# A mixture-of-experts stage: a side computation tied to its written places in the queues, its vectors on GpSimd alone, and two more weight buffers

## The chip, the cores and the metric

One core of one Trainium2 chip runs the whole program. The metric is device time in microseconds (us) from launch to end, the median of several runs. Times inside the program are counted from the start of the profiled span.

## The reference, cut to what matters

The program is two transformer-like blocks over 512 tokens of width 1024. The first block ends in a mixture of 16 experts in which each expert picks its 64 best tokens. The second block has an attention layer, two feed-forward layers and a state-space layer (S5). The part that the change touches is the mixture, and the S5 layer's constant operators, which depend on weights alone and are computed while the mixture runs:

```python
def expert_choice_moe(h, p):
    B, T, D = h.shape
    cap = EC_CAPACITY * T // N_EXPERTS
    affinity = jax.nn.softmax((h @ p['router_w']).astype(jnp.float32), axis=-1)
    gates, idx = lax.top_k(jnp.swapaxes(affinity, 1, 2), cap)
    xe = jax.vmap(lambda hb, ib: hb[ib])(h, idx)
    hid = jax.nn.silu(jnp.einsum('becd,edf->becf', xe, p['exp_w1'])) * jnp.einsum('becd,edf->becf', xe, p['exp_w3'])
    ye = jnp.einsum('becf,efd->becd', hid, p['exp_w2']) * gates[..., None].astype(h.dtype)
    return jax.vmap(lambda ib, yb: jnp.zeros((T, D), yb.dtype).at[ib.reshape(-1)].add(yb.reshape(-1, D)))(idx, ye)
```

Everything is float32. The three weight matrices of the 16 experts are 384 tiles of 128x2048, 1 MB each, and every one is used once.

## The kernel before, in words

`moe` (L1515) takes the experts in eight pairs (`j` from 0 to 7; the text counts them from one, so pair two is `j == 1`). A pair needs 48 weight tiles. The first 32 belong to its **up phase**: two experts, four blocks `fb` each, four tiles `kq` to a block; TensorE multiplies the 64 gathered tokens by each tile (L1588), ScalarE evacuates the block (L1599), four transposes (L1540) and two VectorE operations (L1544, L1545) make the gated hidden layer. Between the tiles of the first expert stand eight matmuls that add the pair before into the output (`combine`, L1552), between those of the second the gather of the next pair's tokens (L1508). The last 16 tiles are the pair's **down phase** (L1620), eight steps `q` of two tiles.

The weight tiles come in one after the other on SyncE's queue (`pair_weight`, L1330, and L1533). Each goes into the next buffer of a ring, and SyncE's queue stands still until the matmuls that read the tile before it in that buffer are done. Pair one has 15 buffers. When it is over they are given up except for six, so pairs two and three have six; from pair four on, `late` adds six more and the tiles go to the two pools in turn.

`s5_prep` (L2013) is a Python generator that writes the S5 operators' work piece by piece: two exponentials and two sines, nine powers of a complex number, squares, a division (all on 128x32 elements, VectorE and ScalarE), and then for each of eight groups `q` the `vectors` (some 20 element-wise operations on up to 128x576 elements that make `CA`, `W` and `bd`) and the `products` (TensorE: two sets of four transposes of `W`, L2110, and one set of matmuls of `CA` and `bd`, L2118; each evacuated by ScalarE and, for `W`, stored to memory). The vectors of even groups are on VectorE (tiles `cuv`, `bigv`, `Wincv`, `bbdv`), those of odd groups on GpSimd (`cug`, `bigg`, `Wincg`, `bbdg`). `moe` takes a piece at twelve points of a pair, from pair two on, and whatever is left at the start of pair four.

The written place of a piece binds nothing: a scheduler at build time sorts each engine's instructions by its own estimate of when they are ready. The engines then work through their queues strictly in order. What the S5 pieces make is first read long after the mixture, in the second feed-forward stretch.

Of the kernel before, what the change touches and what calls it, by code (L numbers as in the profile page):

```python
# [28 lines left out]
NEXP, DEXP, CAP = 16, 2048, 64  # L29
DFF = 2816  # L30
TWO_PI = 2.0 * math.pi
MAGIC = 12582912.0
# [145 lines left out]
class K:  # L178
# [148 lines left out]
    def mod_cols(self, src, which, dst, bias, pool, gate=None, post=None, tags=("wa",)):  # L327
# [26 lines left out]
        if gate is not None:  # L354
            a, row = gate
            g = dst[:, a:a + 8]
            if post is not None:
                t = pool.tile([P, 8], F32, name="gcl", bufs=1)
                V.tensor_tensor(t, g, post, op=OP.mult)
                g = t  # L360
            pt = self.psum(self.mtag, 2)
            nc.tensor.transpose(pt[:8, :P], g, self.ident)
            r = pool.tile([8, P], F32, name="grw8", bufs=1)
            nc.scalar.activation(r, pt[:8, :P], AF.Copy)
            nc.gpsimd.dma_start(row, r)

    def background(self, *parts):
# [1147 lines left out]
    def moe(self):  # L1515
        nc, I = self.nc, self.I
        NJ = NEXP // 2
        with self.mes:
            with ExitStack() as es:
# [3 lines left out]
                nxt = next(g0)  # L1523
                prep, late, acc, MG = (), None, None, None
                turn = cycle(range(2))

                def weight(x):
                    if j == 0:
                        return self.first_w[x] if x < len(self.first_w) else self.pair_weight(j, x)
                    if late is None or next(turn):  # L1530
                        return self.pair_weight(j, x)
                    w = late.tile([P, 2048], F32, name="we", tag="we", bufs=6)
                    nc.sync.dma_start(w, self.weight_src(j, x))  # L1533
                    return w

                def gated(hs, hT, fb):
# [29 lines left out]
                for j in range(NJ):  # L1566
                    XG = nxt
                    last = j == NJ - 1
                    if j == 3:
                        for _ in prep:  # L1570
                            pass
                        s5s.close()
                        late = self.pool(es, "late", side="right")
                    hid = []
                    for e in range(2):
# [4 lines left out]
                        for fb in range(4):  # L1580
                            ps = self.psum("mm", 2)
                            for kq in range(4):
                                next(g0, 0)
                                w = weight(16 * e + 4 * fb + kq).rearrange("p (a b c) -> p a b c", a=2, b=2)
                                for i in range(2):
                                    k = 2 * kq + i
                                    for h in range(2):
                                        nc.tensor.matmul(ps[64 * h:64 * h + 64], XG[:, k, CAP * e:CAP * e + CAP], w[:, i, h],  # L1588
                                                         start=(k == 0), stop=(k == KD - 1), skip_group_check=True)
                                if kq == 0:  # L1590
                                    run()
                                    if e:
                                        nxt = next(gat, None) or nxt
                                else:
                                    next(comb, None)
                                if j and (kq == 0 or kq == 2 and fb % 2):
                                    next(prep, None)
                            hs = wk.tile([P, 512], F32, name="hs")
# [13 lines left out]
                    for q in range(8):  # L1612
# [3 lines left out]
                        for i in range(2):  # L1616
                            f = 2 * q + i
                            for n in range(2):
                                for h in range(2):
                                    nc.tensor.matmul(py[n][64 * h:64 * h + 64], hid[h][:, f], ww[h][:, i, 512 * n:512 * n + 512],  # L1620
                                                     start=(f == 0), stop=(f == 15), skip_group_check=True)
                        if q == 0:
# [8 lines left out]
                    if j == 0:  # L1631
# [7 lines left out]
                        for n in range(2):  # L1639
# [5 lines left out]
                            nc.scalar.activation(MG[:, 512 * n:512 * n + 512], pg, AF.Copy)  # L1645
                        if "D" in self.dbg:
                            prep = self.s5_prep(self.pool(s5s, "s5p", side="right"))
                            next(prep)
# [363 lines left out]
    def s5_prep(self, wk):  # L2012
# [14 lines left out]
        def t32(name):  # L2027
            return wk.tile([P, NPR], F32, name=name)
        are, aim = a[:, 0], a[:, 1]
        dt, dec, th, sn, cn, hp = t32("dt"), t32("dec"), t32("th"), t32("sn"), t32("cn"), wk.tile([P, 1], F32, name="hp")  # L2030
        rw = wk.tile([P, 3, NPR], F32, name="rho")
# [4 lines left out]
        nc.scalar.activation(dec, dec, AF.Exp)  # L2036
        V.tensor_tensor(th, aim, dt, op=OP.mult)
        self.sin_reduce(th, wk, [P, NPR], "s")
        V.memset(hp, math.pi / 2)
        nc.scalar.activation(sn, th, AF.Sin)  # L2040
        nc.scalar.activation(th, th, AF.Abs)
        nc.scalar.activation(cn, th, AF.Sin, scale=-1.0, bias=hp)
        pw = wk.tile([P, 2, 9, NPR], F32, name="pw")
        V.memset(pw[:, 0, 0], 1.0)
# [4 lines left out]
        for j in range(2, 9):  # L2049
            for o, sub in ((0, True), (1, False)):  # L2050
                V.tensor_tensor(t1, pw[:, 0, j - 1], pw[:, o, 1], op=OP.mult)
                V.tensor_tensor(t2, pw[:, 1, j - 1], pw[:, 1 - o, 1], op=OP.mult)
                V.tensor_tensor(pw[:, o, j], t1, t2, op=OP.subtract if sub else OP.add)
        pk = wk.tile([P, 2, 8, NPR], F32, name="pk")
        V.tensor_copy(pk[:, 0], pw[:, 0, 1:])
        V.tensor_scalar(pk[:, 1], pw[:, 1, 1:], -1.0, None, op0=OP.mult)
        nc.scalar.dma_start(self.s5p[:, 0:512], pk.rearrange("p r j n -> p (r j n)"))

        self.square(V, (cn, sn), (t1, t2), wk)
        self.square(V, (t1, t2), (cn, sn), wk)  # L2060
        self.square(V, (cn, sn), (rw[:, 1], rw[:, 2]), wk)
        nc.scalar.dma_start(self.s5p[:, 512:], rw.rearrange("p a n -> p (a n)"))
        den, nr, cre, cim = t32("den"), t32("nr"), t32("cre"), t32("cim")
        V.tensor_tensor(den, are, are, op=OP.mult)
        V.tensor_tensor(t1, aim, aim, op=OP.mult)
        V.tensor_tensor(den, den, t1, op=OP.add)
        V.reciprocal(den, den)
        V.tensor_scalar(nr, pw[:, 0, 1], 1.0, None, op0=OP.subtract)
        ni = pw[:, 1, 1]
        V.tensor_tensor(t1, nr, are, op=OP.mult)  # L2070
# [9 lines left out]
        for q in range(0, NPR, 16):  # L2080
            s = slice(q, q + 16)
            self.cmul((V, G)[q // 16], wk, bb[:, 0, s, None], bb[:, 1, s, None], [v[:, s, None, None] for v in (cre, cim)],
                 [b[:, r, s, None, :] for r in range(2)], [P, 16, 1, 16])
        KT = wk.tile([P, KD, 8, 16], F32, name="KT", tag="sb")

        def vectors(q):

            E, t = ((V, "v"), (G, "g"))[q % 2]
            s = slice(NQ * q, NQ * q + NQ)
# [33 lines left out]
        yield  # L2123
        ops = None
        for q in range(KD + 1):
            new = vectors(q) if q < KD else None
            yield
            if ops is not None:
                yield from products(q - 1, *ops)
            ops = new  # L2130
        nc.gpsimd.dma_start(self.s5k[:, :, 112:].rearrange("q p x -> p q x"), KT.rearrange("p q j c -> p q (j c)"))
# [247 lines left out]
```

## Time and profile before

| what | us |
|---|---|
| median of 3 runs | 3420.55 (3420.32 to 3424.09) |
| the profiled execution, its own time | 3418.57 |
| its span, first to last instruction | 3416.5 |
| pair one of the mixture begins (first L1588) | 984.2 |
| pair two begins | 1103.35 |
| pair two's up phase ends, down phase begins | 1252.38 |
| pair three begins | 1290.86 |
| the last expert's last weight matmul | 2011 |

The core's 16 DMA engines carry all transfers. In most of the mixture they move 421 GB/s, which is a 1 MB (1.0486 MB) weight tile every 2.49 us. TensorE's granted clock is given as a share of 2.4 GHz: 1.00 is 2.4 GHz, 0.50 is 1.2 GHz.

### The profile page before, as it was taken

The page shows a single profiled execution, that of the slowest core. Times are in us where ns is not written, and L with a number is a line of the kernel's source. Part 1 is how long each engine was busy: PE and PEld are TensorE (multiplying, and loading weights), DVE is VectorE, ACT ScalarE, POOL GpSimd, SP SyncE. Part 2 cuts the span into 40 slices and gives each one's busy share as a digit, 9 for nine tenths or more (in the row PEclk, how much of TensorE's full clock was granted, in tenths as well). Part 3 has the DMA queues.
Part 4 walks back from the last instruction along what each step waited for, and adds up shares of the span by engine and source line. Part 5 has one row for each costly group of instructions (what it writes and reads, how often), then busy time and mean ns, then how long its engine had stood idle before and what let it go on. Part 6 is the DMA issues. An engine that isn't in the chain of part 4 may idle for free.

```text
span 3416.5 us, 41161 instructions
## 1 busy us (share of the span) xinstructions
PE 3156.0 (92%) x15981; PEld 1962.0 (57%) x15981; DVE 1727.5 (51%) x3088; ACT 961.3 (28%) x1799; POOL 688.6 (20%) x721
## 2 busy tenths in 40 slices
PE   8988999999999689999999989899888998999999
PEld 3746566666564233333333247565767777778887
DVE  3656767665451911101110136786577775556464
ACT  3314444443221111011001022236332332234242
POOL 1022234432110720000000023210496002210000
PEclk9999989899899899999999999789999998999999
DMA  5643211111659689999999965310336465422221
GB/s 216 240 162 113 66 44 47 44 38 65 246 217 380 242 307 414 419 421 421 421 421 421 421 259 187 111 68 1 120 130 205 164 216 139 152 81 96 96 99 68
DMA packets 144586, 681.34 MB, mean 199 GB/s; under 512 B 25455, under 2 KB 33815, under 8 KB 76424
## 3 DMA queue, kind: packets, MB, share of 16 engines
q1 hardware_dynamic: 134480, 652.47, 50.1%
q0 software_dynamic: 5536, 18.16, 1.4%
q10 hardware_dynamic: 4376, 8.09, 0.7%
q8 instruction: 126, 2.06, 0.2%
q14 instruction: 68, 0.56, 0.1%
HBM read 654.54 MB, written 24.12 MB: 199 GB/s over the span
## 4 chain that ended last, share of the span: by engine, by line
PE 39%; DMA 19%; POOL 7%; DVE 7%; issue 2%; ACT 2%; SPq 0%; POOLq 0%; ACTq 0%; DVEq 0%
DMA we<-in_w_dram 18%; PE mm L1588 5%; PE mm L284 5%; PE mm L285 5%; PE mm L286 5%; POOL cug L2000 3%; PE ch L1620 2%; POOL sca L2001 2%; PE sm L286 1%; PE sm L285 1%; PE sm L284 1%; PE tr L1508 1%; DMA wa<-in_adaw_dram 1%; PE ch L284 1%; PE ch L286 1%
## 5 line engine op out<-in xcount | busy, mean ns | idle before, releaser
L1588 PE MATMUL mm<-we,XG 128*64 128x512 f32 x2048 | 482.6, 609 | 4.6 <-DMA we<-in_w_dram 3.7
L284 PE MATMUL mm<-hh,wh 128*128 128x512 f32 x704 | 281.9, 401 | 21.0 <-DVE vg L1954 16.5
L1588 PEld LDWEIGHTS mm<-we,XG 128*64 128x64 f32 x2048 | 135.4, 138 | 278.8 <-issue 255.4
L1620 PE MATMUL ch<-we,hid 128*64 128x512 f32 x1024 | 267.0, 600 | 16.8 <-DMA we<-in_w_dram 16.7
L285 PE MATMUL mm<-hl,wh 128*128 128x512 f32 x704 | 277.9, 395 | 0.0
L286 PE MATMUL mm<-hh,wl 128*128 128x512 f32 x704 | 272.4, 395 | 0.0
L1544 DVE SCALAR_TENSOR_TENSOR hth<-hth,tr 128x256 f32<-128x256 f32 x64 | 26.9, 420 | 399.5 <-ACT hth L1543 398.9
L1620 PEld LDWEIGHTS ch<-we,hid 128*64 128x64 f32 x1024 | 96.4, 136 | 180.2 <-issue 131.8
L1557 DVE TENSOR_TENSOR acc<-acc,sm 128x512 f32<-128x512 f32 x48 | 33.0, 687 | 305.4 <-PE sm L1552 305.4
L284 PEld LDWEIGHTS mm<-hh,wh 128*128 128x128 f32 x704 | 134.3, 191 | 63.7 <-issue 27.3
L346 DVE SCALAR_TENSOR_TENSOR macc<-wa,cvs,macc 128x512 f32<-128x512 f32 (+1 forms) x119 | 153.6, 1306 | 17.7 <-DMA wa<-in_adaw_dram 15.6
L1669 POOL TENSOR_TENSOR ess<-ess,mhalf 128x1 f32<-128x1 f32 x4 | 2.9, 716 | 786.5 <-DVE ess L1668 786.4
L1599 ACT ACTIVATE hs<-mm 128x512 f32<-128x512 f32 x64 | 38.2, 597 | 415.5 <-PE mm L1588 402.6
L279 DVE TENSOR_TENSOR wl<-wu,wh 128x1024 fp32r<-128x1024 f32 x88 | 115.4, 1313 | 75.2 <-ACT wh L278 74.9
L286 PEld LDWEIGHTS mm<-hh,wl 128*128 128x128 f32 x704 | 134.2, 191 | 29.4
L285 PEld LDWEIGHTS mm<-hl,wh 128*128 128x128 f32 x704 | 134.7, 191 | 26.8 <-POOL hl L455 0.5
L461 POOL TENSOR_TENSOR X<-X,gy 128x512 f32<-128x512 f32 x20 | 28.2, 1430 | 589.3 <-DVE gy L1686 589.2
L278 ACT ACTIVATE wh<-wu 128x1024 fp32r<-128x1024 f32 x88 | 93.3, 1060 | 129.4 <-PE mm L285 96.7
L279 DVE TENSOR_TENSOR wl<-wd,wh 128x1024 fp32r<-128x1024 f32 (+1 forms) x48 | 56.1, 1171 | 96.2 <-ACT wh L278 96.2
L284 PE MATMUL mm<-hTh,wh 128*128 128x512 f32 x208 | 90.4, 435 | 6.5 <-ACT th L795 5.5
L278 ACT ACTIVATE wh<-wd 128x1024 fp32r<-128x1024 f32 (+1 forms) x48 | 47.5, 989 | 164.9 <-PE sm L286 75.0
L286 PE MATMUL mm<-hTh,wl 128*128 128x512 f32 x208 | 89.7, 431 | 2.8 <-DVE wl L279 2.8
(845 smaller groups left out, 6787.7 us busy)
## 6 DMA issues: line engine op xcount, KB each, us to landing
we<-in_w_dram SPq DMA_DIRECT2D x384, 1024.0 KB, 19.8
wu<-in_wupf_dram SPq DMA_DIRECT2D x44, 1024.0 KB, 4.8
wa<-in_adaw_dram SPq DMA_DIRECT2D x24, 1024.0 KB, 4.9
wa<-in_adaw_dram SPq DMA_DIRECT2D x96, 256.0 KB, 4.2
wa<-in_modw_dram SPq DMA_DIRECT2D x16, 1024.0 KB, 6.2
wd<-in_wdn_dram SPq DMA_DIRECT2D x16, 1024.0 KB, 4.8
aw<-in_awin_dram SPq DMA_DIRECT2D x12, 1024.0 KB, 4.9
wi<-in_win_dram SPq DMA_DIRECT2D x46, 256.0 KB, 2.6
```

Of the source, the lines that this page charges most:

```text
L278: self.nc.scalar.activation(h, x, AF.Copy)
L279: (E or self.nc.vector).tensor_tensor(l, x, h.bitcast(F32), op=OP.subtract)
L284: mm(ps, a[0], b[0], start=start, stop=False)
L285: mm(ps, a[0], b[1], start=False, stop=False)
L286: mm(ps, a[1], b[0], start=False, stop=stop)
L346: V.scalar_tensor_tensor(a, w, c, a, op0=OP.mult, op1=OP.add)
L1508: nc.tensor.matmul(ps[:, c * i:c * i + c], self.xn[:, t, o:o + P], oh[:, t], start=(t == 0), stop=(t == TT - 1), skip_group_check=True)
L1588: nc.tensor.matmul(ps[64 * h:64 * h + 64], XG[:, k, CAP * e:CAP * e + CAP], w[:, i, h], start=(k == 0), stop=(k == KD - 1), skip_group_che ...
L1599: nc.scalar.activation(hs, ps, AF.Copy)
L1620: nc.tensor.matmul(py[n][64 * h:64 * h + 64], hid[h][:, f], ww[h][:, i, 512 * n:512 * n + 512], start=(f == 0), stop=(f == 15), skip_group ...
L2000: E.tensor_tensor(u[k], p[k][1], p[k][0], op=OP.mult)
L2001: E.tensor_tensor(o, u[0], u[1], op=op)
```

## The change

A new helper, `pinned`, makes what is traced inside it queue behind a given instruction on that instruction's engine, or behind the last instruction traced so far on a named engine. `moe` takes each S5 piece through it: behind the matmul just written on TensorE, and behind the last instruction written on VectorE and ScalarE. GpSimd is not tied. The points rise from twelve to twenty a pair (sixteen in the up phase, four in the down phase), and the rest is taken at the start of pair six, not four. `s5_prep` is cut into more pieces: eleven for the scalar part, and for each group the vectors, five points at which nothing is written, then three pieces of products; the next group's vectors come with the third. All vectors, and both halves of `bb` before them, are on GpSimd. The ring of weight buffers has eight places in pairs two to five (six, and two of a pool `mid`) and twelve in pairs six to eight (those and four of `late`).

```diff
+    def pinned(self, *behind):
+        es = ExitStack()
+        traced = self.nc.cur_bb.bb.instructions
+        for e in behind:
+            es.enter_context(self.tc.issue_after(next(i for i in reversed(traced) if i.engine == e) if isinstance(e, EP) else e.ins))
+        return es
...
-                turn = cycle(range(2))
...
-                    if late is None or next(turn):
+                    home = next(homes)
+                    if home is None:
                         return self.pair_weight(j, x)
-                    w = late.tile([P, 2048], F32, name="we", tag="we", bufs=6)
+                    w = home[0].tile([P, 2048], F32, name="we", tag="we", bufs=home[1])
...
+                def step(gen, mm):
+                    with self.pinned(mm, EP.DVE, EP.Activation):
+                        return next(gen, None)
...
-                    if j == 3:
+                    if j == 5:
                         for _ in prep:
                             pass
                         s5s.close()
                         late = self.pool(es, "late", side="right")
+                        homes = cycle((None,) * 6 + ((mid, 2),) * 2 + ((late, 4),) * 4)
...
-                                if j and (kq == 0 or kq == 2 and fb % 2):
-                                    next(prep, None)
+                                if j and kq % 2 == 0:
+                                    step(prep, mm)
...
+                        if j and q % 2:
+                            step(prep, mm)
...
                         if "D" in self.dbg:
+                            mid = self.pool(es, "mid", side="right")
+                            homes = cycle((None,) * 6 + ((mid, 2),) * 2)
                             prep = self.s5_prep(self.pool(s5s, "s5p", side="right"))
...
-            self.cmul((V, G)[q // 16], wk, bb[:, 0, s, None], bb[:, 1, s, None], [v[:, s, None, None] for v in (cre, cim)],
+            self.cmul(G, wk, bb[:, 0, s, None], bb[:, 1, s, None], [v[:, s, None, None] for v in (cre, cim)],
...
-            E, t = ((V, "v"), (G, "g"))[q % 2]
+            E, t = G, "g"
...
-        ops = None
-        for q in range(KD + 1):
-            new = vectors(q) if q < KD else None
-            yield
-            if ops is not None:
-                yield from products(q - 1, *ops)
-            ops = new
+        for q in range(KD):
+            ops = vectors(q)
+            for _ in range(5):
+                yield
+            yield from products(q, *ops)
```

Beside these, eight further `yield` lines, one of them in a loop, cut the scalar part of `s5_prep`. The program's line numbers move by 9 to 26.

TensorE's queue in the up phase of pair two, before. `mm<-we,XG` are the weight matmuls, `sm<-ye` the combine, `tr<-misc,hs` the gating, `pp` the S5 products (`Winc`: transposes, `big`: matmuls):

```order
L1552 MATMUL sm<-ye,Gt 128x512
L1588 MATMUL mm<-we,XG 64x512 x3
L2110 MATMUL pp<-misc,Wincv 128x128 x4
L1588 MATMUL mm<-we,XG 64x512
L1552 MATMUL sm<-ye,Gt 128x512
L1588 MATMUL mm<-we,XG 64x512 x4
L1540 MATMUL tr<-misc,hs 128x128 x4
L2110 MATMUL pp<-misc,Wincv 128x128 x4
L1486 MATMUL sm<-gf,misc 128x64 x2
L1588 MATMUL mm<-we,XG 64x512 x4
L2118 MATMUL pp<-bigv,bbdv 32x128 x8
L2110 MATMUL pp<-misc,Wincg 128x128 x4
```

The same queue now, from the end of the up phase of pair two through its down phase (`ch<-we,hid`) into pair three:

```order
L1603 MATMUL mm<-we,XG 64x512 x12
L1554 MATMUL tr<-misc,hs 128x128 x4
L1635 MATMUL ch<-we,hid 64x512 x16
L2138 MATMUL pp<-misc,Wincg 128x128 x4
L1635 MATMUL ch<-we,hid 64x512 x16
L2138 MATMUL pp<-misc,Wincg 128x128 x4
L1635 MATMUL ch<-we,hid 64x512 x16
L2146 MATMUL pp<-bigg,bbdg 32x128 x8
L1635 MATMUL ch<-we,hid 64x512 x16
L1566 MATMUL sm<-ye,Gt 128x512
```

Before, all eight groups' products stand within the up phase of pair two, up to three sets between two weight tiles. Now none stands there: the first group's three sets are in pair two's down phase, four weight tiles apart, and the last group's are in the up phase of pair five.

VectorE's queue in the up phase of pair two, before (`cuv`, `bigv`, `Wincv` are vectors, `acc` the combine, `hth` and `hid` the gating):

```order
L2001 TENSOR_TENSOR bigv<-cuv_7999,cuv_8001 128x4x9x16
L1545 SCALAR_TENSOR_TENSOR hid<-hth,tr 128x256
L2000 TENSOR_TENSOR cuv_8004<-scc,pw 128x576
L2000 TENSOR_TENSOR cuv_8006<-scc,pw 128x576
L1555 COPY acc<-sm 128x512
L2001 TENSOR_TENSOR bigv<-cuv_8004,cuv_8006 128x4x9x16
L2000 TENSOR_TENSOR cuv_8009<-bb,pw 128x512
L2000 TENSOR_TENSOR cuv_8011<-bb,pw 128x512
L1555 COPY acc<-sm 128x512
L2001 TENSOR_TENSOR Wincv<-cuv_8009,cuv_8011 128x4x8x16
```

The same engine now, from the last of the scalar part (in the up phase of pair two) into the up phase of pair three:

```order
L2105 TENSOR_TENSOR cim<-cim,den 128x32
L1558 SCALAR_TENSOR_TENSOR hth<-hth,tr 128x256
L1559 SCALAR_TENSOR_TENSOR hid<-hth,tr 128x256
L1558 SCALAR_TENSOR_TENSOR hth<-hth,tr 128x256
L1559 SCALAR_TENSOR_TENSOR hid<-hth,tr 128x256
L1558 SCALAR_TENSOR_TENSOR hth<-hth,tr 128x256
L1559 SCALAR_TENSOR_TENSOR hid<-hth,tr 128x256
L1558 SCALAR_TENSOR_TENSOR hth<-hth,tr 128x256
L1559 SCALAR_TENSOR_TENSOR hid<-hth,tr 128x256
L2150 SCALAR_TENSOR_TENSOR KT<-misc,cols,KT 128x16
L1571 TENSOR_TENSOR acc<-acc,sm 128x512 x5
```

After the scalar part VectorE has one small S5 operation a group (`KT`); the vectors are gone to GpSimd's queue, where nothing else stands during the mixture.

## Rows read from the trace of the kernel before

**Rows 1.** The span in 40 slices of 85.4 us: busy tenths, GB/s moved.

```profile
PE   8988999999999689999999989899888998999999
DMA  5643211111659689999999965310336465422221
GB/s 216 240 162 113 66 44 47 44 38 65 246 217 380 242 307 414 419 421 421 421 421 421 421 259 187 111 68 1 120 130 205 164 216 139 152 81 96 96 99 68
```

**Rows 2.** Busy time by stretch: length, each engine's us, PEclk, DMA share, GB/s.

```profile
1125.00:1145.00 20.00, 12.73 (x42) 4.35 (x43) 19.85 (x18) 2.17 (x4) 19.37 (x14) 0.74 0.40 144
...
1225.00:1252.00 27.00, 25.55 (x158) 13.30 (x155) 1.92 (x5) 5.84 (x14) 1.00 (x1) 1.00 0.89 323
1252.00:1400.00 148.00, 138.12 (x600) 52.27 (x600) 14.67 (x31) 12.42 (x27) 0.00 (x0) 1.00 1.00 411
1400.00:2000.00 600.00, 562.00 (x2443) 207.80 (x2440) 67.98 (x141) 57.20 (x122) 0.00 (x0) 1.00 1.01 421
```

**Rows 3.** What TensorE waited for from 1103 to 1253: total us, times, longest.

```profile
PE pp L2110 <- POOL Wincg L2001: 17.9, 4, 8.4
PE sm L1552 <- DVE acc L1555: 7.4, 1, 7.4
PE pp L2110 <- DVE Wincv L2001: 4.3, 3, 2.8
```

**Rows 4.** TensorE in order of time, pair two: start, us, line, tiles, count.

```profile
1103.35 1.94 PE L1588 MATMUL mm<-we,XG 128*64 128x512 f32 x8
...
1197.22 1.11 PE L2110 MATMUL pp<-misc,Wincg 128*128 128x128 f32 x4 [8.44 <-POOL Wincg L2001]
...
1210.65 0.66 PE L2110 MATMUL pp<-misc,Wincv 128*128 128x128 f32 x4 [0.69 <-ACT sst L2112]
...
1213.11 1.13 PE L2118 MATMUL pp<-bigv,bbdv 128*32 128x128 f32 x16
```

**Rows 5.** TensorE in order of time, pairs two to four and eight.

```profile
1252.38 11.29 PE L1620 MATMUL ch<-we,hid 128*64 128x512 f32 x48
...
1290.86 1.94 PE L1588 MATMUL mm<-we,XG 128*64 128x512 f32 x8
...
1374.82 16.73 PE L1620 MATMUL ch<-we,hid 128*64 128x512 f32 x68
...
1411.64 1.94 PE L1588 MATMUL mm<-we,XG 128*64 128x512 f32 x8
```

**Rows 6.** GpSimd in order of time, the vectors of groups three, five and seven.

```profile
1155.15 1.74 POOL L2001 TENSOR_TENSOR bigg<-cug,cug 128x576 f32<-128x576 f32 x1 [6.72 <-PE pp L2118]
...
1181.71 1.43 POOL L2001 TENSOR_TENSOR bigg<-cug,cug 128x576 f32<-128x576 f32 x1 [3.72 <-PE pp L2118]
...
1194.75 2.41 POOL L2001 TENSOR_TENSOR Wincg<-cug,cug 128x512 f32<-128x512 f32 x1
...
1207.07 1.42 POOL L2001 TENSOR_TENSOR bigg<-cug,cug 128x576 f32<-128x576 f32 x1 [2.47 <-PE pp L2118]
...
1208.70 2.96 POOL L2000 TENSOR_TENSOR cug<-scc,pw 128x576 f32<-128x576 f32 x2
...
1216.90 1.28 POOL L2001 TENSOR_TENSOR Wincg<-cug,cug 128x512 f32<-128x512 f32 x1
```

**Rows 7.** VectorE in order of time: the same operation in even groups.

```profile
1127.85 2.62 DVE L2000 TENSOR_TENSOR cuv<-scc,pw 128x576 f32<-128x576 f32 x2
...
1150.20 1.43 DVE L2000 TENSOR_TENSOR cuv<-scc,pw 128x576 f32<-128x576 f32 x2
```

**Rows 8.** DMA from 1093 to 1260: queue, packets, MB, share; issues, KB, landing us.

```profile
q10 hardware_dynamic: 2592, 4.51, 7.1%
q0 software_dynamic: 464, 1.62, 2.5%
...
we<-in_w_dram SPq DMA_DIRECT2D x39, 1024.0 KB, 6.2
...
s5k<-KT POOLq DMA_DIRECT2D x1, 512.0 KB, 8.0
```

More of the change, by code (lines that the diff above doesn't have):

```diff
@@ L30 @@
 DFF = 2816
+EP = mybir.EngineType
 TWO_PI = 2.0 * math.pi
@@ L1523, in moe @@
                 nxt = next(g0)
-                prep, late, acc, MG = (), None, None, None
-                turn = cycle(range(2))
+                prep, late, acc, MG = iter(()), None, None, None
                 def weight(x):
@@ L1587, in moe @@
                                     for h in range(2):
-                                        nc.tensor.matmul(ps[64 * h:64 * h + 64], XG[:, k, CAP * e:CAP * e + CAP], w[:, i, h],
-                                                         start=(k == 0), stop=(k == KD - 1), skip_group_check=True)
+                                        mm = nc.tensor.matmul(ps[64 * h:64 * h + 64], XG[:, k, CAP * e:CAP * e + CAP], w[:, i, h],
+                                                              start=(k == 0), stop=(k == KD - 1), skip_group_check=True)
                                 if kq == 0:
@@ L1619, in moe @@
                                 for h in range(2):
-                                    nc.tensor.matmul(py[n][64 * h:64 * h + 64], hid[h][:, f], ww[h][:, i, 512 * n:512 * n + 512],
-                                                     start=(f == 0), stop=(f == 15), skip_group_check=True)
+                                    mm = nc.tensor.matmul(py[n][64 * h:64 * h + 64], hid[h][:, f], ww[h][:, i, 512 * n:512 * n + 512],
+                                                          start=(f == 0), stop=(f == 15), skip_group_check=True)
+                        if j and q % 2:
+                            step(prep, mm)
                         if q == 0:
@@ L2037, in s5_prep @@
         V.tensor_tensor(th, aim, dt, op=OP.mult)
+        yield
         self.sin_reduce(th, wk, [P, NPR], "s")
         V.memset(hp, math.pi / 2)
+        yield
         nc.scalar.activation(sn, th, AF.Sin)
@@ L2042, in s5_prep @@
         nc.scalar.activation(cn, th, AF.Sin, scale=-1.0, bias=hp)
+        yield
         pw = wk.tile([P, 2, 9, NPR], F32, name="pw")
@@ L2053, in s5_prep @@
                 V.tensor_tensor(pw[:, o, j], t1, t2, op=OP.subtract if sub else OP.add)
+            if j % 2 == 0:
+                yield
         pk = wk.tile([P, 2, 8, NPR], F32, name="pk")
@@ L2057, in s5_prep @@
         nc.scalar.dma_start(self.s5p[:, 0:512], pk.rearrange("p r j n -> p (r j n)"))
+        yield
         self.square(V, (cn, sn), (t1, t2), wk)
@@ L2062, in s5_prep @@
         nc.scalar.dma_start(self.s5p[:, 512:], rw.rearrange("p a n -> p (a n)"))
+        yield
         den, nr, cre, cim = t32("den"), t32("nr"), t32("cre"), t32("cim")
@@ L2068, in s5_prep @@
         V.tensor_scalar(nr, pw[:, 0, 1], 1.0, None, op0=OP.subtract)
+        yield
         ni = pw[:, 1, 1]
@@ L2123, in s5_prep @@
         yield
-        ops = None
-        for q in range(KD + 1):
-            new = vectors(q) if q < KD else None
-            yield
-            if ops is not None:
-                yield from products(q - 1, *ops)
-            ops = new
+        for q in range(KD):
+            ops = vectors(q)
+            for _ in range(5):
+                yield
+            yield from products(q, *ops)
         nc.gpsimd.dma_start(self.s5k[:, :, 112:].rearrange("q p x -> p q x"), KT.rearrange("p q j c -> p q (j c)"))
```

## The prediction

> **What bounds the kernel now.** I read the slices of the whole span first, to see where the mixture is limited. From the sixteenth slice to the twenty-second the DMA digit is 9 and the core moves 414 to 421 GB/s; in the two slices before (1110 to 1281 us) the digits are 6 and 9 at 242 and 307 GB/s [rows 1]. So the mixture is bound by its weight stream except where the S5 pieces run. The stretches say the same more finely: 144 GB/s from 1125 to 1145 us with the clock at 0.74, against 421 GB/s from 1400 to 2000 us [rows 2]. There VectorE or GpSimd is busy throughout and TensorE is not. The waits name the cause: within pair two TensorE stood 17.9 us before S5 transposes whose `Wincg` GpSimd had not finished, 4.3 us for VectorE's `Wincv`, and 7.4 us before a combine whose accumulator operation stood in VectorE's queue behind vectors [rows 3]. Weight matmuls that need nothing of S5 stand behind these in TensorE's queue, as at 1197.22, after 8.44 us of waiting [rows 4]. When TensorE stands, no weight buffer comes free, SyncE's queue stands, and the DMA engines run dry. The time that counts is thus the weight stream's: each microsecond in which it stops is lost for good, since it has no reserve later.
>
> **The change, part by part.**
>
> *The S5 pieces leave pair two's up phase.* Before, that phase lasts from 1103.35 [rows 4] to 1252.38 [rows 5], 149.0 us. The same 32 tiles, with combine and gather and without S5, take 84.0 us in pair three (1290.86 to 1374.82) [rows 5]. The new queue has no S5 product in pair two's up phase, so it should take those 84.0 us: minus 65.0 us. The 65 us hold the waits above, the products themselves, and matmuls at the lower of the clock's two levels (1.2 and 2.4 GHz; 0.74 is a mean of both); all of it goes with the idling.
>
> *Two more buffers.* SyncE has issued as many tiles as TensorE has used, plus the ring. At the end of the up phase that is 32 + 6 before and 32 + 8 after, and from there on the stream runs without a pause (411 and 421 GB/s [rows 2]). Two tiles ahead at 2.49 us are minus 5.0 us. Bounds: 0, if a later full ring eats the lead, and minus 5.0; I take 5.0, since the stretch before the stream becomes continuous shows it slot-bound (323 GB/s [rows 2]).
>
> *S5's own transfers now share a full stream.* Before, they lay in pair two's half-empty stretch and cost nothing. From pair two's down phase on each takes time from the weights. ScalarE's queue moved 4.51 MB [rows 8]; at 421 GB/s that is 10.7 us, by its share of the DMA engines 7.1% of 167 us, 11.9 us. The final store of 512 KB is 1.2 us more, and 0.3 MB of powers (0.7 us) stay in the up phase. Bounds 11.2 and 12.4; I take plus 12.
>
> *The products on TensorE.* Per group two sets of transposes at 0.66 and one of matmuls at 1.13 us [rows 4], 2.45, times eight is 19.6 us, now in pairs two to five. TensorE is busy 562 of 600 us in the steady part [rows 2], so it has 7.6 us of slack in a pair of 48 tiles or 119.5 us, 26 us over the 3.4 pairs that hold S5 work (68 points, twenty a pair), and S5's transfers give it another 12. On average they are covered. Not everywhere: a pair's up phase is the tight part (32 tiles at 2.49 are 79.7 us, against 84.0 on TensorE), and there a full ring stops the stream. Pair three before shows what that costs with six buffers: 411 instead of 421 GB/s over 148 us [rows 2], 3.5 us. That loss is in the time I carry over. With S5 in three up phases it may come again once or twice: 0 to 7 us, I take plus 4.
>
> *The scalar part on VectorE and ScalarE.* It now lies in eleven pieces between the combines of pair two, where VectorE waits for ScalarE's sines and a combine can stand behind. The nearest row is a wait of TensorE for a ScalarE evacuation, 0.69 us [rows 4]; none to four of these are 0 to 3 us, I take plus 2.
>
> *All vectors on GpSimd.* This costs nothing only while GpSimd finishes before TensorE asks. From the first operation that waits for the products before to the end of the first `Winc` it took 15.5 us in group five (1181.71 to 1197.16) and 11.1 us in group seven (1207.07 to 1218.18), when VectorE had stopped [rows 6]. Now TensorE asks five points later: ten weight tiles in an up phase, at 2.49 us each 25 us, and more where down-phase points lie between. The cover is at least 9 us a group. Without it each group would wait at the head of TensorE's queue as before. Group zero also waits for `bb`, some 10 us more, and has 14 tiles, 35 us.
>
> A rule speaks against this part. A pair of 128x576 products took 1.43 us on VectorE at 1150.20, when GpSimd stood still (6.72 us of waiting up to 1155.15), and 2.96 us on GpSimd at 1208.70, when VectorE had no vectors left [rows 6, 7]. The Trainium skill ("GPSIMD Engine Reference", Engine selection) says to keep element-wise work off GpSimd, as it is about twice as slow for two inputs; the trace agrees. By the rule the change would double the vectors' work; off the path it leaves the sum as it is, and it feeds the second rival.
>
> When both worked, at 1127.85, VectorE's pair took 2.62 us [rows 7]. The skill ("SBUF — State Buffer", SBUF: two separate sides) states an exclusive lock between GpSimd and VectorE operations with two SBUF inputs. The trace agrees in direction; by it GpSimd alone should be nearer 11 than 15 us, which leaves more cover.
>
> *Unchanged.* From pair six on the ring has twelve buffers, as before from pair four, and the stream was full either way.
>
> *Sum.* 65.0 and 5.0 gained, 12, 4 and 2 lost: minus 52 us. The profiled execution took 3418.57, so 3366.5; the median lies 2.0 above it, so **3368 us**. With the bounds: from minus 58.8 (11.2, 0, 0) to minus 42.6 (slots 0 would make it 37.6), 3361 to 3378, and some 2 us each way for the hand-over to the attention stage, where ScalarE's sine table comes in at another place.
>
> **The rivals.**
>
> *One: S5's transfers are free after all*, because TensorE is the limit in the pairs that carry S5 and the stream has gaps to fill. For it: the up phases are TensorE's. Against it: over a whole pair the stream is the longer. Minus 65, 5, plus 2 and 2: 3354 us.
>
> *Two, the other side: GpSimd becomes the head of TensorE's queue.* Eight groups in line on one engine, each twice as slow as on VectorE. It decides from the point where the first `Winc` takes over 25 us. To be slower than before it must eat 52 us, 6.5 a group: over 32 us where the slowest row has 15.5 [rows 6]. At 36 us a group it would lose 11 times eight, 88 us, less 52: 3456 us. Against it: nothing but vectors is in that queue, and VectorE now hardly competes.
>
> *Three: the tied queues wait in small steps.* Three sets a group, each with ScalarE and VectorE behind it in fixed order; where one is late, gating and combine stand behind. One and a half waits of 0.69 us [rows 4] for each of the 24 sets, none of them covered, are 25 us more: 3393 us. Against it: sets lie two or four tiles apart, and each evacuation has that long.
>
> *Four: the change doesn't do what it says.* The tie holds a piece back but doesn't hurry it, and the queues show the pieces where they are written. What could remain is that the stream stops for another reason in this stretch. 3420 us.
>
> **How the numbers follow.** Forecast (3359 to 3382) 0.68, rival one 0.08, rival three 0.13, rival four 0.05, rival two and other losses 0.06. Range: from a little below rival one to rival three's figure, 3352 to 3393, which leaves out rivals two and four and the edges. Within 0.2%, 6.8 us, is about what a measurement of this kernel can't tell from no change: faster 0.89, same 0.05, slower 0.06.
>
> **What would show it.** Right: pair two's up phase at 84 to 88 us; no wait of TensorE for `Wincg`; the clock at 1.00 from pair two on; 400 GB/s or more from pair two's down phase; GpSimd at work in separate blocks of 15 us through pair five; the last weight matmul near 1958 us. Wrong: GB/s under 380 in pairs three to five (rival three, or two if `Wincg` is named in the waits); an up phase of pair two over 95 us, which means that its scalar pieces cost more than I allow; or a stage after the mixture that has moved by more than 5 us, which I don't expect from the queues.

## The result, and the profile after

The changed kernel took 3371.0 us, median of 4 runs (3367.8 to 3376.9), against 3422.3 of the kernel before (4 runs, 3420.3 to 3424.1): ratio 0.985, 95% interval 0.984 to 0.987. The forecast was 3368 us. A second measurement, beside the last two experiments, gave 3363.0 (median of 5 runs) against 3426.0 (9 runs): ratio 0.981, interval 0.978 to 0.983.

The slices of the span answer to [rows 1]. Columns are slices of 84 us.

```profile
PEclk9998989889789999999999999789998998999999
DMA  5643211101559999999999954210336456322221
GB/s 219 233 167 119 67 35 57 48 32 45 200 215 394 369 421 421 421 421 420 420 421 421 420 201 162 101 57 24 117 122 234 156 195 163 132 88 91 97 100 69
```

The two slices that stood at 242 and 307 GB/s are gone: after 394 and 369 the stream is at 420 or 421 to the end of the mixture. The stretches of pair two's up phase, its down phase, pairs three to five, and pairs six to eight answer to [rows 2] (length, busy time of PE, PEld, DVE, ACT and POOL with counts, PEclk, DMA share, GB/s):

```profile
1109.00:1191.00 82.00, 77.39 (x368) 30.05 (x368) 25.45 (x111) 14.29 (x30) 26.08 (x30) 1.00 0.99 408
1191.00:1229.00 38.00, 36.90 (x157) 13.54 (x158) 2.04 (x3) 2.84 (x6) 8.96 (x11) 1.00 1.01 420
1229.00:1599.00 370.00, 351.73 (x1672) 136.68 (x1670) 48.70 (x94) 46.47 (x100) 102.29 (x107) 1.00 1.01 421
1599.00:1950.00 351.00, 328.02 (x1415) 118.10 (x1414) 40.34 (x83) 31.96 (x68) 0.00 (x0) 1.00 1.01 420
```

The clock is at 1.00 in all of them, and GpSimd's 102 us of vectors lie under a full stream. What TensorE waited for from 1109 to 1600 us (total, times, longest) answers to [rows 3]:

```profile
PE tr L1554 <- ACT hs L1614: 17.4, 24, 0.8
PE ch L1635 <- DMA we<-in_w_dram: 6.0, 9, 1.0
```

No `Wincg`, no `acc`. (`hs` is ScalarE's evacuation of a block, which the gating's transposes read.) TensorE in order of time (start, us, line, tiles, count) answers to [rows 4, 5]: the first and last weight products, where pairs two, three and six begin, and the first S5 products:

```profile
989.87 3.68 PE L1603 MATMUL mm<-we,XG 128*64 128x512 f32 x8 [0.62 <-ACT XG L1521]
...
1109.00 1.94 PE L1603 MATMUL mm<-we,XG 128*64 128x512 f32 x8
...
1191.48 7.14 PE L1635 MATMUL ch<-we,hid 128*64 128x512 f32 x32
1198.55 0.65 PE L2138 MATMUL pp<-misc,Wincg 128*128 128x128 f32 x4
...
1218.43 1.14 PE L2146 MATMUL pp<-bigg,bbdg 128*32 128x128 f32 x16
...
1229.56 1.94 PE L1603 MATMUL mm<-we,XG 128*64 128x512 f32 x8
...
1249.41 0.66 PE L2138 MATMUL pp<-misc,Wincg 128*128 128x128 f32 x4
...
1598.96 1.94 PE L1603 MATMUL mm<-we,XG 128*64 128x512 f32 x8
...
1955.53 3.65 PE L1635 MATMUL ch<-we,hid 128*64 128x512 f32 x12 [0.56 <-DMA we<-in_w_dram]
```

Two more rows of the kernel before, the first and last of its weight products, give the mixture as a whole:

```profile
984.17 2.83 PE L1588 MATMUL mm<-we,XG 128*64 128x512 f32 x6 [0.62 <-ACT XG L1512]
...
2007.77 3.65 PE L1620 MATMUL ch<-we,hid 128*64 128x512 f32 x12 [0.53 <-DMA we<-in_w_dram]
```

The mixture lasted 1027.2 us and now lasts 969.3 (from the first start to the last end), 57.9 less. The span lost 50.7 (3416.5 to 3365.8). The other 7.2 are stages that the change doesn't touch: the mixture began 5.7 us later, and what follows it took 1406.6 instead of 1405.1 us. Since the mixture's start moves from run to run (below), the table compares the kernels by stage, each from its own single trace; phases are counted as in the prediction (from the first product of one to the first of the next).

| kernel | mixture starts | pair two's up phase | pairs three to five | mixture | median, us |
|---|---|---|---|---|---|
| before | 984.2 | 149.0 | 361.0 | 1027.2 | 3422.3 |
| changed | 989.9 | 82.5 | 369.4 | 969.3 | 3371.0 |
| changed, again | 999.2 | 82.5 | 369.3 | 968.7 | 3363.0 |
| changed, no tie | 995.0 | 164.5 | 359.9 | 1065.5 | 3466.4 |
| before, tie alone | 996.0 | 105.5 | 372.4 | 993.5 | 3390.5 |
| ring of six | 990.5 | 83.6 | 377.6 | 978.4 | 3377.2 |
| ring of six, two engines | 997.4 | 92.0 | 378.5 | 986.5 | 3382.5 |
| one point, not five | 984.5 | 97.4 | 408.7 | 1025.9 | 3428.6 |
| stores doubled | 993.0 | 82.5 | 385.0 | 986.9 | 3380.3 |
| stores on GpSimd's queue | 995.7 | 82.5 | 370.5 | 966.9 | 3367.1 |
| the same, again | 991.4 | 82.5 | 370.5 | 966.7 | 3361.8 |
| doubled, GpSimd's queue | 995.0 | 82.5 | 379.2 | 975.8 | 3375.2 |

### The profile page after: what moved, and what is told of

Same layout as the page of the kernel before. It is cut to its first block, busy times and chain, and to the rows that moved or that the text cites. A ratio compares the mean times of both kernels' runs of the same rounds, so it can differ in the third digit from the quotient of the medians.

```text
span 3365.8 us, 41149 instructions
## 1 busy us (share of the span) xinstructions
PE 3142.1 (93%) x15981; PEld 1959.1 (58%) x15981; DVE 1660.9 (49%) x3014; ACT 962.8 (29%) x1799; POOL 740.8 (22%) x795
## 4 chain that ended last, share of the span: by engine, by line
PE 46%; DMA 14%; POOL 6%; DVE 6%; issue 2%; ACT 2%; SPq 0%; POOLq 0%; ACTq 0%; DVEq 0%
DMA we<-in_w_dram 13%; PE mm L1603 9%; PE mm L285 5%; PE mm L286 5%; PE mm L287 5%; PE ch L1635 3%; POOL cug L2019 3%; PE tr L1517 2%; POOL sca L2020 2%; PE sm L287 1%; PE sm L286 1%; PE sm L285 1%; PE sm L1566 1%; PE ch L286 1%; PE ch L285 1%
## 5 line engine op out<-in xcount | busy, mean ns | idle before, releaser
L1603 PE MATMUL mm<-we,XG 128*64 128x512 f32 x2048 | 473.5, 601 | 3.9 <-DMA we<-in_w_dram 3.1
L1558 DVE SCALAR_TENSOR_TENSOR hth<-hth,tr 128x256 f32<-128x256 f32 x64 | 26.9, 421 | 393.9 <-ACT hth L1557 393.4
```

Source lines behind the costliest of these rows:

```text
L1603: mm = nc.tensor.matmul(ps[64 * h:64 * h + 64], XG[:, k, CAP * e:CAP * e + CAP], w[:, i, h], start=(k == 0), stop=(k == KD - 1), skip_grou ...
```

## The experiments

### Is it the tie?

First run: the changed kernel, the tie taken out.

```diff
 def step(gen, mm):
-    with self.pinned(mm, EP.DVE, EP.Activation):
-        return next(gen, None)
+    return next(gen, None)
```

> The changed kernel with the tie alone taken out: the same points, the vectors all on GpSimd, the same eight buffers, but a step's instructions no longer have to stand behind the weight product and the last vector and scalar instruction written before them. In the order all eight products then stand in pair two, three to five weight tiles apart. Theory (the tie is what takes the pieces out of pair two, and with one engine for all the vectors a kernel without it is worse than the one before): GpSimd needs about 15 us for each of eight operators, one after the other, so TensorE waits for Wincg in pair two, 40 to 60 us in all, and the stream stops behind it: pair two 160 to 180 us instead of 120, total about 3415 (3395 to 3445). Rival (the tie is a formality, the gain comes from the points and the buffers): no wait for Wincg over 3 us, 3368 to 3378.

3466.4 us, ratio 1.012 (1.008 to 1.015): slower than before. The direction is that of the theory, the size is not. TensorE's waits from 1112 to 1345 us, two stretches of pair two, its first and last waits for `Wincg`, and the group of GpSimd's work that waited (busy, mean ns, idle before it and the releaser):

```profile
PE pp L2137 <- POOL Wincg L2019: 63.9, 8, 14.1
```

```profile
1145.00:1180.00 35.00, 20.58 (x80) 7.60 (x80) 3.16 (x7) 3.08 (x7) 26.39 (x26) 0.66 0.25 89
1180.00:1220.00 40.00, 21.55 (x101) 7.05 (x100) 4.08 (x6) 4.06 (x9) 30.87 (x34) 0.75 0.51 198
```

```profile
1149.73 1.11 PE L2137 MATMUL pp<-misc,Wincg 128*128 128x128 f32 x4 [14.14 <-POOL Wincg L2019]
...
1312.33 1.12 PE L2137 MATMUL pp<-misc,Wincg 128*128 128x128 f32 x4 [7.17 <-POOL Wincg L2019]
```

```profile
L2019 POOL TENSOR_TENSOR bigg<-cug,cug 128x576 f32<-128x576 f32 x16 | 22.6, 1414 | 46.6 <-PE pp L2145 46.4
```

The waits (63.9 us) lie just above the expected 40 to 60. But pair two took 227.5 us, not 160 to 180: from the first group's wait to the last's, the rows above, it is 162.6 us, seven steps of 23.2 and not of 15. GpSimd stood 46.4 us itself, before it might overwrite `bigg`, until TensorE had done the group's products (L2145), and these stood behind weight products. Each waited for the other in turn. TensorE also worked at a mean clock of 0.66 and 0.75, and its own work took longer: four transposes 1.11 us, where the changed kernel's took 0.65. My estimate had only one of the two directions. This is the prediction's rival two with its mechanism: `Wincg` heads TensorE's queue, at a distance of three to five tiles.

Second run: the kernel before, the tie put in, nothing else.

```diff
-                                if j and (kq == 0 or kq == 2 and fb % 2):
-                                    next(prep, None)
+                                if j and (kq == 0 or kq == 2 and fb % 2):
+                                    step(prep, mm)
```

> The kernel before with the tie alone put in: the old points (three of four in the up phases), vectors in turn on VectorE and GpSimd, one operator ahead, ring of six, second ring from pair four. In the order the products then lie over the up phases of pairs two and three, about four weight tiles to an operator. Theory: the tie carries most of the gain. What is missing is the spread of the scalar part, which is still one piece of some 33 us ahead of the first Wincv, so TensorE waits 10 to 25 us once, early in pair two; later waits are under 3 us each; total about 3393 (3382 to 3405). Rival A (the spread over more points and the buffers are what counts): 3410 to 3422. Rival B (the tie is all of it): 3368 to 3377.

3390.5 us, ratio 0.990 (0.988 to 0.993), and the mixture 993.5 us: 33.7 of the 57.9 us. What is missing is where it was expected, in pair two's up phase (105.5 against 82.5 us). TensorE's waits from 1112 to 1400 us hold one for `Wincv`, behind the scalar part that is still written in one piece:

```profile
PE pp L2124 <- DVE Wincv L2015: 10.9, 1, 10.9
PE tr L1554 <- ACT hs L1613: 9.1, 12, 1.4
```

That is 10.9 of the 23.0 us; what the rest of them is, no run separates. So the tie is the core of the change. Alone it brings 33.7 us of the mixture; everything else without it costs 38.3 (1065.5 against 1027.2).

### The five points

```diff
             ops = vectors(q)
-            for _ in range(5):
-                yield
+            yield
             yield from products(q, *ops)
```

> The changed kernel with one point instead of five between an operator's vectors and its first product; all else, the tie too, as it is. Theory (the five points are the cover for GpSimd's chain of 11 to 15 us, 25 us of it): with one point, 5 us, TensorE waits for Wincg in most of the eight operators, 5 to 10 us each, 40 to 70 us in all; the eight buffers take up some 20 us once, and the rest is lost, since TensorE gains only 0.16 us a tile on the stream; total 3395 to 3430, about 3412, the products over by pair three. Rival (the vectors come so early that the distance does not count): waits under 3 us each, 3368 to 3378.

3428.6 us, ratio 1.001 (0.9995 to 1.003): all of the gain is gone. The theory holds; the total, and with it the mixture (56.6 us more), lies at the upper edge of what I gave. The waits from 1112 to 1620 us, and two stretches of 100 us with the S5 pieces in them:

```profile
PE pp L2138 <- POOL Wincg L2020: 43.0, 8, 7.2
```

```profile
1145.00:1245.00 100.00, 83.83 (x410) 34.68 (x410) 10.41 (x40) 12.14 (x26) 58.17 (x64) 0.91 0.88 351
1245.00:1345.00 100.00, 74.38 (x339) 26.65 (x332) 16.88 (x28) 11.77 (x24) 64.42 (x68) 0.86 0.79 298
```

Eight waits, one to a group, 7.2 us the longest, and the mixture lost more than their 43.0 us; the mean clock fell with them, to 0.86. With one point the groups also follow each other after three points instead of seven; how much of the other 13.6 us is the clock and how much the closer products, no run separates. At too short a distance the tied pieces give back all that the tie brought (mixture 1025.9 us, 1027.2 before).

### The two buffers

```diff
-    mid = self.pool(es, "mid", side="right")
-    homes = cycle((None,) * 6 + ((mid, 2),) * 2)
+    homes = cycle((None,))
...
-    homes = cycle((None,) * 6 + ((mid, 2),) * 2 + ((late, 4),) * 4)
+    homes = cycle((None,) * 6 + ((late, 6),) * 6)
```

> The changed kernel without the two added buffers: ring of six in pairs two to five, six more from pair six. Theory (the buffers are worth 0 to 5 us): the mixture, 969 us, becomes 969 to 974, total 3371 to 3376; short waits of TensorE for a weight tile appear behind the products. Rival (it is the longer ring that carries the lumps which the products make in TensorE's queue): waits for weights of 1 to 2 us at most of the 24 products, the mixture 985 or more, total 3387 or more.

3377.2 us, mixture 978.4: 9.1 us more than the changed kernel (9.7 by its second trace), beyond the 5 us that I had as the upper bound, short of the rival's 16. Only 1.2 us of it lie in pair two's up phase, where I had seen the lead of two tiles; 8.3 lie in pairs three to five, over which the stream ran at 412 GB/s, where the changed kernel has 421:

```profile
1231.00:1608.00 377.00, 354.79 (x1668) 136.04 (x1668) 48.72 (x94) 45.97 (x99) 101.66 (x107) 1.00 1.01 412
```

A close look at the end of pair three's up phase, where gather and S5 products stand together, shows the stop (two stretches of 5 us, and the later one in the changed kernel, where the same tiles stand 1.4 us earlier):

```profile
1310.00:1315.00 5.00, 5.00 (x32) 2.60 (x32) 0.00 (x0) 1.50 (x4) 4.82 (x5) 1.00 0.99 388
1315.00:1320.00 5.00, 4.24 (x24) 1.51 (x22) 0.84 (x2) 0.98 (x2) 1.03 (x1) 1.00 0.91 336
```

```profile
1315.00:1320.00 5.00, 4.24 (x22) 1.67 (x21) 0.84 (x2) 0.98 (x2) 0.00 (x0) 1.00 1.01 421
```

TensorE falls behind the stream there and SyncE's queue waits for its matmuls (19.1 us in seven waits from 1300 to 1325): six buffers are full, and the stream stops; with eight it doesn't. At two of the four later places where the stream fell under 400 GB/s (in stretches of 5 us), SyncE also waited 3.3 or 3.6 us for a store to land (more on this below), so not all of the 8.3 us need be TensorE's.

### GpSimd alone, or both engines

```diff
-            E, t = G, "g"
+            E, t = ((V, "v"), (G, "g"))[q % 2]
```

> The ring-of-six form of the changed kernel with the vectors (and the two halves of bb) in turn on VectorE and GpSimd, tied, the five points kept; to be read against the ring-of-six run (mixture 978.4 us, total 3377.2), since the second set of tiles does not fit beside the added buffers. Theory (term f: the engine that makes the vectors is off the path): mixture 976 to 981 us, no wait for either Winc tile. Rival A (VectorE's 8 to 15 us blocks stand ahead of the mixture's own vector work, as the wait for acc of 7.4 us before): waits for acc, oh or XG of 5 us or more, four times, mixture 985 to 1000. Rival B (GpSimd's longer chain did cost something): mixture 972 or less.

3382.5 us, mixture 986.5, 8.1 more than the ring of six with GpSimd alone. That is rival A, at its lower edge: one wait, not four. It came in pair two's up phase (92.0 against 83.6 us). TensorE and VectorE in order of time there:

```profile
1181.34 1.19 PE L1517 MATMUL tr<-oh,xn 128*128 128x128 f32 x4 [5.63 <-DVE hid L1559]
```

```profile
1175.65 3.09 DVE L2018 TENSOR_TENSOR cuv<-bb,pw 128x512 f32<-128x512 f32 x2
1178.66 0.41 DVE L1558 SCALAR_TENSOR_TENSOR hth<-hth,tr 128x256 f32<-128x256 f32 x1
```

The gating operation (L1558) stood behind group zero's vectors, and the gather of TensorE behind the gating. The clock of 1165 to 1185 us fell to 0.83. No wait for either `Winc` tile came up, so GpSimd's slower vectors cost nothing, while giving half the groups to the faster engine cost 8 us, through this one wait and the lower clock around it: the slower engine is the better place here.

### What S5's transfers cost

The sixteen stores issued twice, the second time to a place that nobody reads:

```diff
                 nc.scalar.dma_start(self.s5i[q, :, r], st.rearrange("p (i c) -> p i c", c=P))
+                nc.scalar.dma_start(self.s5j[q, :, r], st.rearrange("p (i c) -> p i c", c=P))
```

> The changed kernel with each of the sixteen 256 KB stores of the operators' inputs issued a second time, into a tensor that nobody reads. Theory (the stream sets the pace from pair two on, so S5's transfers cost their bytes): 4.2 MB more at 421 GB/s is 10 us; the mixture becomes 977 to 982 us, total about 3381 (3378 to 3386). Rival one of the prediction (such transfers are free beside the stream): the mixture stays within 2 us, total 3369 to 3373. A third case, that the stores cost more than their bytes because the weight queue waits for their landings: 990 us or more, total 3392 or more.

3380.3 us in total, as the theory says; but the mixture is 986.9, 17.6 more, which is neither the 10 us of the bytes nor the third case's 21. The weight queue's waits from 1112 to 1620 us say where more could come from (total, times, longest): those for landings of stores, first in the changed kernel and then here.

```profile
SPq L1339 <- DMA s5i<-sst: 75.5, 13, 8.4
SPq L1542 <- DMA s5i<-sst: 19.5, 3, 8.2
```

```profile
SPq L1339 <- DMA s5i<-sst: 71.1, 10, 11.6
SPq L1339 <- DMA s5j<-sst: 25.7, 11, 4.2
SPq L1542 <- DMA s5i<-sst: 23.5, 3, 11.6
SPq L1542 <- DMA s5j<-sst: 5.8, 3, 2.7
```

SyncE's queue holds weight loads, but it stood until stores had landed that ScalarE's queue had issued, 95 us in the changed kernel and 126 here. To tell waits from bytes, all of S5's stores were moved to GpSimd's queue, once as they are and once doubled:

```diff
-                nc.scalar.dma_start(self.s5i[q, :, r], st.rearrange("p (i c) -> p i c", c=P))
+                nc.gpsimd.dma_start(self.s5i[q, :, r], st.rearrange("p (i c) -> p i c", c=P))
```

> The changed kernel with the stores of pk, rho and the sixteen operator inputs issued from GpSimd's queue instead of ScalarE's; the same bytes. In the changed kernel the weight queue stood for 95 us in 16 waits on the landings of these sixteen stores and 14 us on the other two, while the stream kept 421 GB/s. Theory (eight buffers cover these waits; what S5's transfers cost is their bytes): mixture within 3 us of 969, total 3368 to 3375, whether the waits stay or go. Rival (the waits on landings are part of the price): they go, and the mixture shortens by 4 to 8 us, total 3363 to 3367.

> Each operator store issued twice, as in the fourth run (mixture 986.9 us, which is 17.7 more, of which 10.0 are the bytes at 421 GB/s; 410 GB/s in pairs three to five), but all S5 stores from GpSimd's queue. Theory (the other 7.7 us is the weight queue standing for landings of up to 11.6 us, longer than the ring covers): with the stores on another queue these waits go, the stream is back at 420 GB/s, the mixture is 978 to 981 us, total about 3373 to 3378. Rival (a byte written costs more of the stream than a byte read, 1.8 times): the stream stays near 410 GB/s and the mixture at 985 to 989 us.

The waits for S5 landings are gone from the weight queue in both. Doubled, the mixture is 975.8 us, 8.9 more than with single stores on the same queue (966.9), against 10.0 by the bytes, and 11.1 less than doubled on ScalarE's queue. Pairs three to five of the doubled stores, on ScalarE's queue and on GpSimd's:

```profile
1235.00:1620.00 385.00, 359.73 (x1669) 136.56 (x1668) 48.72 (x94) 46.24 (x99) 101.73 (x107) 0.99 1.01 413
```

```profile
1233.00:1612.00 379.00, 356.56 (x1670) 136.20 (x1668) 48.59 (x94) 46.27 (x99) 116.49 (x134) 1.00 1.01 421
```

So a written byte costs about what a byte read does, and the rest was the weight queue's standing, where it was too long for the ring: single waits of 9.2 to 11.6 us stand at four places in pairs three to five where the stream with doubled stores on ScalarE's queue fell under 380 GB/s, again in stretches of 5 us. The mixture of 975.8 us came out below the 978 to 981 that I gave, since the single stores had become cheaper too: 966.9, 2.4 us less than the changed kernel and within the theory's 3. In the changed kernel itself the stop shows once: where SyncE waited 8.8 us for the store of `pk`, the stream fell to 311 GB/s, while with the stores on GpSimd's queue it kept 421:

```profile
1145.00:1155.00 10.00, 9.24 (x46) 3.18 (x44) 4.74 (x31) 0.98 (x2) 0.46 (x1) 1.00 0.83 311
```

```profile
1145.00:1245.00 100.00, 94.97 (x452) 37.70 (x448) 15.79 (x63) 12.15 (x26) 44.41 (x51) 1.00 1.01 421
```

Over 10 us, 110 GB/s less is 1.1 MB, 2.6 us of the stream. I ran both once more, side by side.

> The changed kernel as it is, once more, beside the form with S5's stores on GpSimd's queue. Theory (the mixture repeats closely; what moves from run to run is the work ahead of it, whose first weight product came between 984 and 997 us in the nine traces so far): mixture 968 to 971 us, its start anywhere from 984 to 998, total 3366 to 3378. Rival (the later start in the changed kernel's first trace is an effect of the change): the start at 990 plus or minus 1.

> The form with all S5 stores on GpSimd's queue, once more, on the same chip as the changed kernel itself. Theory (waits on landings are worth 2 to 3 us here, since they stopped the stream once or twice, near the start of pair two and in its down phase): mixture 966 to 968 us, total 2 to 4 us under the changed kernel's of this call. Rival (the first run's 2.3 us were chance): mixture within 1 us of the changed kernel's, totals within their spread.

The mixtures are 968.7 and 966.7 us, after 969.3 and 966.9 the first time: 2.0 and 2.4 less, and pair two's down phase alone is 2.5 and 2.6 us shorter: the tiles that the stop held back are missing there. The wait for `pk` is 8.8 us in the changed kernel's second trace too. The changed kernel's mixture now started at 999.2, so the rival that the change moved the start to 990 is out; this start and the total, 3363.0, lie outside the ranges I gave. The totals, 3363.0 (3353.5 to 3369.6) and 3361.8 (3358.1 to 3374.2), don't tell the two apart, and the 2 to 4 us that I expected between them did not show. By the traces the stores belong on GpSimd's queue, but the totals show no faster kernel.

## Why the prediction was right, step by step

**Pair two's up phase.** Forecast 84.0 us, minus 65.0; measured 82.5, minus 66.5. The comparison with pair three [rows 5] was the right one: with the ring of six, as pair three had it, the phase takes 83.6. The plus 2 for the scalar pieces did not show: TensorE's short waits are those for `hs`, 0.8 us at most.

**The two buffers: the mis-sized term.** Forecast minus 5.0 with 5.0 as the upper bound; the ring-of-six run says minus 9.1. I counted a lead, two tiles at the end of pair two's up phase, and put what a full ring costs, plus 4, into a term of its own that eight buffers would not change. But the lead is 1.2 us, and the stops of a full ring are what the buffers take away: 412 to 421 GB/s in pairs three to five. The row for it was there, 411 GB/s in pair three [rows 2], read as a loss that is carried over. Without the buffers the sum was minus 47, and the ring-of-six run gave minus 48.8: the term that was mis-sized is this one.

**S5's transfers.** Forecast plus 12. Pairs three to five took 8.4 us longer than the same pairs before (369.4 against 361.0), and the doubled stores 8.9 for 10.0 by bytes. The mechanism, bytes on a full stream, holds, and at 8.9 us for 4.2 MB the 5.0 MB of [rows 8] (ScalarE's queue and the last store) come to 10.7 us, a little under the forecast. Rival one, free transfers, is excluded.

**GpSimd's cover.** It held. GpSimd in order of time for group one, whose start waits for group zero's products:

```profile
1219.78 1.42 POOL L2020 TENSOR_TENSOR bigg<-cug,cug 128x576 f32<-128x576 f32 x1 [37.39 <-PE pp L2146]
...
1221.41 2.40 POOL L2019 TENSOR_TENSOR cug<-scc,pw 128x576 f32<-128x576 f32 x2
...
1229.06 1.28 POOL L2020 TENSOR_TENSOR Wincg<-cug,cug 128x512 f32<-128x512 f32 x1
```

From 1219.78 to 1230.34 it is 10.6 us to the first `Winc`, and TensorE asked at 1249.41. In [rows 6] it was 11.1 to 15.5. The pair of 128x576 products took 2.40 us against VectorE's 1.43 in [rows 7].

The Trainium skill ("SBUF — State Buffer", SBUF: two separate sides) states a lock that GpSimd and VectorE hold against each other. The trace agrees in direction: with VectorE's vectors gone, the chain of 10.6 us is nearer 11 than 15, as the prediction had it. The Trainium skill ("GPSIMD Engine Reference", Engine selection) says to keep element-wise work with two inputs off GpSimd, as about twice as slow. Here it was 1.7 times as slow, and still half the groups on VectorE made the mixture 8 us longer, since VectorE's queue is one that TensorE waits behind. All groups on VectorE wasn't tried.

**Rivals two and three.** Rival two needs its distance: it came up without the tie and with one point, where it gave 3466 and 3429 us, and not with five. Rival three, small waits in the tied queues, did not show: beside waits for weight tiles, only 17.4 us of waits for `hs` are listed, 24 of 0.8 at most. They are the gating's own, for the kernel before has 21 of them, 14.2 us, in pairs three to five, where it has no S5 products.

**The sum.** Minus 52 forecast for the mixture, minus 57.9 measured (58.5 in its second trace): pair two's up phase gave 66.5 where 63 were summed, and the rest of the mixture took 8.6 us longer where 11 were. The sum had no term for the weight queue's standing for stores, which costs 2.0 to 2.4 us; such waits were there before, 12.5 us in three waits for operator stores from 1103 to 1260 us. And its lower bound is added up wrongly: 65.0 and 5.0 less 12.4, 7 and 3 are 47.6, and without the buffers 42.6; the 37.6 takes the buffers off twice. The times given, 3361 to 3378, are those of 58.8 and 42.6. That the total of the first measurement came within 3 us of the forecast is partly luck: the work ahead of the mixture, for which I expected no change, was 5.7 us longer in that trace than in the one before. The second measurement, 63 us less than before, is nearer to what the stage says.

**What was to show it.** The missing `Wincg`, the clock, the 400 GB/s, the separate blocks of GpSimd and the last weight product (1959 for 1958) came as listed. The up phase, 82.5 us, is a little under the 84 to 88 listed. GpSimd's blocks take 14 us, the second `Winc` included. What follows the mixture took 1.5 us longer; over all twelve traces it lies between 1398.7 and 1409.3 us, so the 5 us that were to be a sign of error are within what it moves by itself.

## What to carry to other kernels

A side computation that is tied to its places in in-order queues is free only if every hand-over between engines has its distance: here 10.6 us of GpSimd's work need more than one point of some 5 us, and with five the slower engine alone beats both engines in turn, since the main work stands behind the faster one's queue. Count ring buffers by the longest time that the consumer, or the queue that refills them, stands still, not by the lead that they give once. And compare stages, not totals, when the work ahead of the stage moves by more from run to run than the term in question.

## What the runs showed of the hardware

Ahead of the mixture the program was the same in all twelve traces, yet the mixture's first weight product came between 984.2 and 999.2 us. The stretch of 300 to 600 us, in the kernel before and in the changed kernel's second trace:

```profile
300.00:600.00 300.00, 277.35 (x1994) 182.59 (x1991) 223.00 (x492) 133.96 (x295) 103.51 (x101) 0.93 0.17 54
```

```profile
300.00:600.00 300.00, 280.08 (x1933) 183.13 (x1930) 215.03 (x471) 131.77 (x287) 98.76 (x97) 0.88 0.16 53
```

TensorE is about as busy, but gets less done in the time (1933 matmuls instead of 1994), at a mean granted clock of 0.88 instead of 0.93. In the changed kernel's mixture the clock was 1.00 in all four stretches from pair two on, and the mixture's length repeated within 0.6 us. What decides the clock ahead of it wasn't tried.

The other surprise is that a queue that only loads weights stood for the landings of stores from another engine's queue, 95 us in 16 waits, and stopped doing so when GpSimd's queue issued them. The semaphores of the traces tell why: this program gives the transfers of SyncE's and ScalarE's queues the same eight semaphores for their landings (99, 101 to 105, 108 and 109), and SyncE waits, before it issues a load, for the last transfer with the same semaphore. In the changed kernel the store of `pk` took 104, landed at 1152.61, and the next weight load, also on 104, was issued at 1152.67. With the stores on GpSimd's queue they have others (111 to 118).
